# Part of the input projection by seven products for eight, ahead of the attention, in a streaming encoder layer

## The chip, the cores and the metric

The kernel runs on one core of a Trainium2 chip. The metric is the device time of one execution in microseconds (us). Engines are named as the profile names them: PE (matrix products; PEld loads its weights), DVE and ACT (elementwise work), POOL (elementwise work and some DMA issues), SP (DMA issues). SBUF is the memory on the chip that the engines read; PSUM holds the products' sums.

## The reference

One layer of an encoder for 592 rows: 64 rows of a running stream (`x_sample`, with 128 cached keys), 16 learned rows (`meta`) and 512 rows of a new stream. Group A has eight heads of differential attention, group B eight heads of latent attention.

```
h   = rmsnorm(x, norm_attn_g)
z   = h @ w_in                  # 2048 -> 3904: q 1024, k 1024, v 1024, cq 512, ckv 256, krope 64
A:  s = q_c . k_c * scale + bias (c = 0, 1);  p = softmax(s_0) - lam * softmax(s_1);  o_d = p @ v
B:  qm = rmsnorm(cq) @ w_uq;  km, vm = rmsnorm(ckv) @ w_ukv;  rotary parts;  softmax;  o_m
x   = x + concat(rmsnorm(o_d) * 0.8, o_m) @ w_out
x   = x + (silu(h2 @ w_gate) * (h2 @ w_up)) @ w_down      # h2 = rmsnorm(x, norm_ffn_g), 5632 wide
y   = rmsnorm(x, final_norm_g)
```

The new keys, values, latents and rotated keys are outputs too. Everything is float32.

## The kernel before

Columns are tokens, rows (128 partitions) are features: x is transposed once and z comes out as 31 blocks of 128 features by 592 tokens: 24 head blocks (q, k, v of heads 0 to 7), four of cq, two of ckv, one of krope written twice. A float32 number is split into a high and a low part in the format (fp32r) in which PE multiplies here (`split`: ACT makes `hi`, DVE `lo = x - hi`), and a product is three: hi.hi, lo.hi, hi.lo (`mm3`). So a block (`project`, L211) is 16 slices of the inner dimension x 3 x 2 token halves of 296 columns = 96 matmuls; its weights come in two DMAs of half a megabyte (`wr`) and are split into `wh`, `wl`.

The phases follow each other. First (L341 to L545) x is loaded token tile by token tile in four groups of columns; each of 16 chunks is transposed on PE (`transpose_x`), scaled by the norm's gain and split into `xh`, `xl`, while q and k of head 0 are already accumulated chunk by chunk, then v; DVE copies of x go to DRAM (`xspill`) for the residual sum. The row norm `rb` is multiplied in when a block is read from PSUM.

Then (to L714) the planner `Streams` (L46) interleaves generators. Each has a rank and a time at which it is ready; of those ready the lowest rank goes next, and `take`/`give` hand out PSUM banks at estimated times. Its order is binding for PE alone, whose instructions are held in program order; the other engines' are ordered by a scheduler. `projections` (rank 9) is what fills PE: q, k, v of a head, then the ckv, kr and cq blocks. Behind it run `keys`, `values` (transposes for the outputs) and `diff_attend` (L588, rank 1): for each of five query blocks and both maps (c = 0, 1) a group of score matmuls into the one bank pair `sp`, a DVE pass that adds the bias and finds the maximum (`nm`), an exponential on ACT (`e`), then the combination; then `probabilities_times_values` (L221). A head's attention starts when the one before it has ended.

Second (L717 to L991), in new rooms, `latents` turns ckv, krope and cq into keys and queries of group B (rotation, norms, splits), `latent_rows` stores the new latents, then eight latent heads run over `mix_out`, group A's half of the output projection, which fills PE. Then come the other half, and the feed-forward part, whose products are already formed by Winograd's scheme for 2 x 2 blocks (seven products and 15 sums instead of eight products), with sums of weights (`ws`) on POOL (L1112) and DVE, and sums of results (`m`) on DVE. The order of seven that this part uses is `CHAIN`; four banks a, b, c, d hold the products.

## Time and profile before

| | |
|---|---|
| median of three runs | 2491.58 us (2489.09 to 2492.69) |
| the profiled execution | 2491.91 us, span 2490.1 us, mean granted clock 0.994 |
| PE busy | 2425.4 us, 97% |
| DVE busy | 1776.4 us, 71% |
| ACT busy | 1122.4 us, 45% |
| POOL busy | 741.2 us, 30% |

All windows and rows that follow are of that profiled execution. A row of the page's groups reads: line, engine, operation, out<-in, shapes, count | total busy us, mean ns of one | idle time before them and what ended it. In a row of the timeline the first two numbers are start and duration, in us; a bracket tells an idle time before it and what ended that. A group made by a helper has the helper's line (L108 matmul, L125 the elementwise engines), so groups are told apart by their tiles' names. Busy times of matmuls overlap, because they are pipelined: what a matmul costs is the distance from one start to the next.

### The profile page before, as it was taken

Reading aid. Unit: us, or ns where it says so; the run is one execution under the profiler, and the core shown is the slowest. Engines: PE = TensorE matmul, PEld = TensorE weight load, DVE = VectorE, ACT = ScalarE, POOL = GpSimd, SP = SyncE. Lnnn points to the kernel's source line nnn. Section 1 sums busy time; section 2 is a strip of 40 time slices with the busy share of each in tenths; the row PEclk is TensorE's granted clock in tenths of the full one; section 3 lists DMA queues with packets and bytes.
Section 4 is the critical chain, followed back from the end, with each engine's and each line's share of the span. In section 5 each row is a group of like instructions: output and inputs, shape, how many; then the busy total and the mean of one; then the engine's idle time right before and its main releaser. Section 6 shows DMA issues by size and latency. Waiting matters only on the chain.

```text
span 2490.1 us, 45138 instructions
## 1 busy us (share of the span) xinstructions
PE 2425.4 (97%) x17865; PEld 2380.8 (96%) x17865; DVE 1776.4 (71%) x2815; ACT 1122.4 (45%) x2142; POOL 741.2 (30%) x598
## 2 busy tenths in 40 slices
PE   8999999998999999999999999999999999999998
PEld 6999999997999888999999999999999999999998
DVE  5555555557556467877888888888788887888874
ACT  5333333334434344445555555455554433333445
POOL 0000000001000066454554544545544422222223
PEclk9999999999999999999999999999999999999999
DMA  7433223325322454234434444344443866645332
GB/s 216 146 91 86 76 79 87 83 65 160 98 86 90 133 160 146 93 121 140 156 119 142 153 140 149 118 148 155 135 144 136 299 221 204 219 156 177 109 111 85
DMA packets 336485, 338.06 MB, mean 136 GB/s; under 512 B 25827, under 2 KB 279658, under 8 KB 336274
## 3 DMA queue, kind: packets, MB, share of 16 engines
q1 hardware_dynamic: 335714, 333.12, 41.9%
q8 instruction: 140, 2.29, 0.4%
q0 software_dynamic: 560, 2.06, 0.2%
q14 instruction: 71, 0.58, 0.1%
HBM read 265.21 MB, written 72.61 MB: 136 GB/s over the span
## 4 chain that ended last, share of the span: by engine, by line
PE 55%; DVE 2%; POOL 1%; DMA 1%; issue 1%; ACT 1%; DVEq 0%; POOLq 0%; SPq 0%
PE m L1143 36%; PE m L1147 18%; PE m L205 1%; DVE wl L125 1%; DMA raw<-in_ffn_w_down 1%; POOL ws L1112 1%; DVE b L125 0%; PE m L1510 0%; DMA raw<-in_ffn_w_gate 0%; ACT b L125 0%; DMA raw<-in_ffn_w_up 0%; DVE ws L125 0%; POOL c L1315 0%; POOL b L1497 0%; DMA b<-sumspill 0%
## 5 line engine op out<-in xcount | busy, mean ns | idle before, releaser
L1143 PE MATMUL m<-b,wh 128*128 128x288 f32 x7168 | 1048.1, 295 | 4.7 <-ACT wh L125 4.3
L1143 PEld LDWEIGHTS m<-b,wh 128*128 128x128 f32 x7168 | 983.9, 188 | 6.7 <-ACT wh L125 5.7
L1147 PE MATMUL m<-b,wl 128*128 128x288 f32 x3584 | 579.9, 297 | 2.4 <-DVE wl L125 2.2
L1112 POOL TENSOR_TENSOR ws<-raw 128x512 f32<-128x512 f32 (+1 forms) x258 | 370.4, 1445 | 543.1 <-DVE wl L125 256.5
L1147 PEld LDWEIGHTS m<-b,wl 128*128 128x128 f32 x3584 | 513.6, 188 | 4.2 <-DVE wl L125 4.1
L125 ACT ACTIVATE wh<-ws 128x512 fp32r<-128x512 f32 (+1 forms) x340 | 283.5, 846 | 391.2 <-PE m L1143 247.7
L125 DVE TENSOR_TENSOR wl<-ws,wh 128x512 fp32r<-128x512 f32 (+1 forms) x340 | 388.5, 1153 | 89.7 <-ACT wh L125 89.5
L125 DVE TENSOR_TENSOR wl<-raw,wh 128x512 fp32r<-128x512 f32 x387 | 357.3, 947 | 7.4 <-ACT wh L125 6.6
L125 ACT ACTIVATE wh<-raw 128x512 fp32r<-128x512 f32 x387 | 227.4, 620 | 286.6 <-PE m L1143 262.0
L108 PE MATMUL ps<-xh,wh 128*128 128x296 f32 x960 | 221.5, 312 | 2.3 <-ACT wh L125 2.3
L108 PE MATMUL ps<-xh,wl 128*128 128x296 f32 x960 | 210.9, 301 | 1.1 <-DVE wl L125 1.1
L108 PE MATMUL ps<-xl,wh 128*128 128x296 f32 x960 | 211.0, 301 | 0.0
L125 DVE TENSOR_TENSOR y<-y,m 128x288 f32<-128x288 f32 x312 | 139.6, 449 | 87.3 <-PE m L1147 67.9
L125 DVE TENSOR_TENSOR ws<-ws,raw 128x512 f32<-128x512 f32 (+1 forms) x129 | 114.2, 888 | 73.3 <-POOL ws L1112 71.3
L108 PEld LDWEIGHTS ps<-xh,wh 128*128 128x128 f32 x960 | 157.3, 191 | 6.8 <-ACT wh L125 3.1
L108 PEld LDWEIGHTS ps<-xh,wl 128*128 128x128 f32 x960 | 157.3, 190 | 2.1 <-DVE wl L125 2.1
L108 PEld LDWEIGHTS ps<-xl,wh 128*128 128x128 f32 x960 | 157.8, 191 | 0.0
L125 DVE TENSOR_TENSOR wl<-wr,wh 128x1024 fp32r<-128x1024 f32 (+1 forms) x110 | 118.2, 1075 | 37.3 <-ACT wh L125 35.6
L125 ACT ACTIVATE wh<-wr 128x1024 fp32r<-128x1024 f32 (+1 forms) x110 | 101.6, 929 | 63.1 <-PE ps L108 52.0
L1315 POOL TENSOR_TENSOR c<-c,rb 128x576 f32<-128x576 f32 x44 | 70.9, 1613 | 168.5 <-ACT c L125 168.5
L591 POOL MEMSET bias<- 64x64 f32 x8 | 1.2, 144 | 396.1 <-DMA bias<-tsk 231.6
L1423 POOL TENSOR_TENSOR c<-c 128x576 f32<-128x576 f32 x42 | 73.7, 1755 | 85.5 <-DVE c L125 80.3
(355 smaller groups left out, 3196.0 us busy)
## 6 DMA issues: line engine op xcount, KB each, us to landing
raw<-in_ffn_w_gate SPq DMA_DIRECT2D x44, 1024.0 KB, 7.2
raw<-in_ffn_w_up SPq DMA_DIRECT2D x44, 1024.0 KB, 6.8
raw<-in_ffn_w_down SPq DMA_DIRECT2D x39, 1024.0 KB, 5.4
partspill<-parts SPq DMA_DIRECT2D x126, 288.0 KB, 2.1
b<-partspill SPq DMA_DIRECT2D x126, 288.0 KB, 5.9
wr<-in_w_in SPq DMA_DIRECT2D x60, 512.0 KB, 4.1
wr<-in_w_out SPq DMA_DIRECT2D x16, 512.0 KB, 4.4
wr<-in_w_out SPq DMA_DIRECT2D x32, 256.0 KB, 3.6
```

Source lines behind the costliest of these rows:

```text
L108: self.tc.keep_in_program_order(self.pe.matmul(out, lhsT, rhs, start=start, stop=stop))
L125: ins = issue(*args, **kwargs)
L205: PE.matmul(outs[i], w, x[i], start=start and p == 0, stop=stop and p == 2)
L591: G.memset(bias[0:64, 464:528], -BIG)
L1112: engine.tensor_tensor(w[:, k:k + m, :], pick(xs), pick(ys), op=op)
L1143: PE.matmul(banks[p], wh[:, k, :], x, start=first and new and k == 0 and x is hi, stop=False, skip_group_check=not new)
L1147: PE.matmul(banks[p], wl[:, k, :], hi, start=False, stop=last and k == n - 1, skip_group_check=not new)
L1315: G.tensor_tensor(g[:, f, :], g[:, f, :], rb2, op=ALU.mult)
L1423: G.tensor_tensor(w[:, f, :], w[:, f, :], g[:, f, :], op=ALU.mult)
```

## The change

Three parts.

*Seven products for eight.* A block pair is seen as 2 x 2: token halves by feature halves of 128, and the inner 2048 split into even and odd chunks. Of the 31 blocks, 17 are projected first, before any attention: q and k of heads 0, 1, 2 (`EARLY`), the eight v in pairs, the two ckv, each pair as a `Product` of 7 x 24 matmuls, and kr as a `Single` of 4 x 24. x is loaded whole, transposed, copied with the gain (`xg`) and without (`xt`, to `xspill`, now whole rows), and the operands of the seven products are built from `xg`: four kinds in rooms that last as x's splits (p = 1, 2, 3, 5) and three others (6, 7, 4). Two pairs run interleaved at first (`START`, in the written order of DVE, ACT and SP too), then the others one behind the other (`run`). The norm `rb` is computed behind them from x loaded once more. The results go to DRAM (`zspill`).

*Heads overlap.* `heads` (rank 5) loads q, k, v of a head again and multiplies by `rb` on POOL where that is due; `projections` (rank 9) has only the q and k of heads 3 to 7 and cq left, 14 blocks, each now in two PSUM tiles of one bank. A head's scores start after the scores of the head before; the two maps have a bank each (`s0`, `s1`), the wide block 3 takes both; the transposes have two banks; probabilities (`pt_b`) have two sets, `e` four, `p5` two.

*Latents in x's room.* The key latents' norm (`key_latents`) runs at the start of the attention. With the last projection x's room (`xk`) is closed and `latents` is spawned in a new pool in that place, so the cosines, the rotation, the queries' norm and the row stores run before the phase ends, and the latent heads start with the next phase at once.

The diff, cut to its core:

```diff
+EARLY = 3
...
-    def project(ps, wsrc, xs, dup=False):
-                mm3([ps[:, 0, 0:TH], ps[:, 1, 0:TH]], wh[:, k, :], wl[:, k, :],
-                    halves(xs[kc][0]), halves(xs[kc][1]), kc == 0, kc == KC - 1)
+    def project(ps, wsrc, xs):
+                for h in ((0,), (1,)) if kc == 0 else ((0, 1),):
+                    mm3([ps[i][:, 0:TH] for i in h], wh[:, k, :], wl[:, k, :],
+                        [hi[i] for i in h], [lo[i] for i in h], kc == 0, kc == KC - 1)
...
+            def transpose_x(kc):
+                cg, k = kc // 4, kc % 4
+                ps = banks()
+                for j, (o, n) in enumerate(tok):
+                    b = o // TH
+                    PE.transpose(ps[:, b, o - b * TH:o - b * TH + n],
+                                 xt_in[cg, j][0:n, k * P:(k + 1) * P], ident[0:n, 0:n])
+                xg[kc] = room((7, 4)[kc % 2], kc // 2)
+                S.activation(xg[kc], ev(ps), AF.Copy, scale=gA[:, kc:kc + 1])
+                xt[kc] = room((6, 5)[kc // 8], kc % 8)
+                V.tensor_copy(xt[kc], ev(ps))
+            def split_operand(p, m, src):
+                t = room(p, m, F32R)
+                operands[p, m] = ends(t)
+                split(*operands[p, m], src)
+            def first_operands(m):
+                (b11, b12), (b21, b22) = ends(xg[2 * m]), ends(xg[2 * m + 1])
+                split_operand(1, m, b11)
+                split_operand(2, m, b21)
+                G.tensor_tensor(b11, b12, b11, op=ALU.subtract)
+            def other_operands():
+                for m in range(PAIRS):
+                    split_operand(3, m, xg[2 * m + 1][:, 1, :])
+                    yield
+                def sums(n):
+                    t = flat(wp.tile([P, 8, P], F32, name="wr", tag="wr", bufs=WR_BUFS))
+                    return [t[:, i * TH:(i + 1) * TH] for i in range(n)]
+                for m in range(PAIRS):
+                    if m % 3 == 0:
+                        c = sums(3)
+                    G.tensor_tensor(c[m % 3], xg[2 * m + 1][:, 1, :], xg[2 * m][:, 0, :], op=ALU.subtract)
+                    split_operand(6, m, c[m % 3])
+                    yield
+                for m in range(PAIRS):
+                    split_operand(5, m, xg[2 * m][:, 0, :])
+                    yield
+                for m in range(PAIRS):
+                    (t5, b12), (b21, b22) = ends(xg[2 * m]), ends(xg[2 * m + 1])
+                    c7, c4 = sums(2)
+                    G.tensor_tensor(c7, b22, b12, op=ALU.subtract)
+                    G.tensor_tensor(c4, b21, b22, op=ALU.subtract)
+                    G.tensor_tensor(c4, c4, t5, op=ALU.add)
+                    split_operand(7, m, c7)
+                    yield
+                    split_operand(4, m, c4)
+                    yield
+            class Product:
...
+                def weights(self, p, early=False):
+                    a11, a12, a21, a22 = (self.a[f, t] for f in range(2) for t in range(2))
+                    if p == 5:
+                        self.sum = src = self.combine(G, a21, a22, ALU.add, self.sum)
+                    elif p == 6:
+                        src = self.sum if early else self.combine(V, self.sum, a11, ALU.subtract, self.sum)
+                    elif p == 3:
+                        if early:
+                            self.sum = self.combine(G, a21, a22, ALU.add)
+                            self.combine(V, self.sum, a11, ALU.subtract, self.sum)
+                        src = self.combine(V, a12, self.sum, ALU.subtract, a12 if early else self.sum)
+                    elif p == 7:
+                        src = self.combine(G, a11, a21, ALU.subtract, a11)
+                    else:
+                        src = {1: a11, 2: a12, 4: a22}[p]
+                    wh = wp.tile([P, 8, P], F32R, name="wh", tag="wh", bufs=WH_BUFS)
+                    wl = wp.tile([P, 8, P], F32R, name="wl", tag="wl", bufs=WH_BUFS)
+                    for i, x in enumerate(src):
+                        split(wh[:, 4 * i:4 * i + 4, :], wl[:, 4 * i:4 * i + 4, :], x)
+                    return wh, wl
+                def multiply(self, p, name, w, first):
+                    wh, wl = w
+                    out = {"a": self.ab[:, 0, 0:TH], "b": self.ab[:, 1, 0:TH],
+                           "c": self.c_[:, 0, 0:TH], "d": self.c_[:, 1, 0:TH]}[name]
+                    self.bank[p] = out
+                    for m in range(PAIRS):
+                        for x in operands[p, m]:
+                            PE.matmul(out, wh[:, m, :], x, start=first and m == 0 and x is operands[p, m][0],
+                                      stop=False, skip_group_check=not first)
+                    for m in range(PAIRS):
+                        PE.matmul(out, wl[:, m, :], operands[p, m][0], start=False, stop=m == PAIRS - 1,
+                                  skip_group_check=not first)
...
+                def run(self, chain, step):
+                    seen = set()
+                    for p, name in chain:
+                        self.multiply(p, name, self.weights(p), name not in seen)
+                        seen.add(name)
+                        self.take(p)
+                        step()
+                    self.keep()
...
+            load_x(0)
+            load_x(1)
+            load(oh, c_onehot)
+            load(rbt, rel_bias)
+            raws = [raw_weights((0, P), (OFF_K, P))]
+            load_x(2)
+            load_x(3)
+            raws.append(raw_weights((P, P), (OFF_K + P, P)))
...
+            first, second = [Product(r, (h, 8 + h)) for h, r in enumerate(raws)]
+            START = [(1, "a", first), (2, "c", first), (1, "a", second), (2, "c", second)]
+            START += [(p, n, c) for p, n in ((3, "d"), (6, "a"), (5, "b"), (7, "a"), (4, "a")) for c in (first, second)]
+            ws = [c.weights(p, True) for p, n, c in START[:2]]
+            for kc in range(KC):
+                store(xspill[kc], flat(xt[kc]))
+            store(trow, trs)
+            building = other_operands()
+            for _ in range(PAIRS):
+                next(building)
+            for i, (p, name, call) in enumerate(START):
+                call.multiply(p, name, ws.pop(0), p not in (6, 7, 4))
+                call.take(p, True)
+                for _ in range(3 + i % 2):
+                    next(building, None)
+                if i + 2 < len(START):
+                    q, _, c = START[i + 2]
+                    ws.append(c.weights(q, True))
...
+            for h in range(2, EARLY):
+                Product(raw_weights((h * P, P), (OFF_K + h * P, P)), (h, 8 + h)).run(CHAIN, step)
+            for h in range(0, H, 2):
+                Product(raw_weights((OFF_V + h * P, 2 * P)), (16 + h, 17 + h)).run(CHAIN, step)
+            Product(raw_weights((OFF_CKV, 2 * P)), (28, 29)).run(CHAIN, step)
+            last = raw_weights((OFF_KR, 64), (OFF_KR, 64))
+            Single(last, (30,)).run(((1, "a"), (2, "c"), (6, "a"), (3, "b")), step)
...
-                    yield from st.take("sp")
-                    n, W, view, vw = scores(b, sbig(), [qs[h % 2][c]], [(kh, kl)])
+                    if b == 3:
+                        sp = yield from take_both()
+                    else:
+                        yield from st.take(f"s{c}")
+                        sp = sbanks[:, c:c + 1, :]
+                    n, W, view, vw = scores(b, sp, [qs[h % 2][c]], [(kh, kl)])
...
+        def projections():
+            for i in [o + h for h in range(EARLY, H) for o in (0, 8)]:
+                ps = pjt()
+                off = i * P if i < 8 else OFF_K + (i - 8) * P
+                yield from project(ps, w_in[:, off:off + P], xs1)
+                z = ztile()
+                normed(z, ps)
+                store(zspill[i], z)
+                projected[i]["done"] = True
+            for i in range(4):
+                off = OFF_CQ + i * P
+                ps = pjt()
+                yield from project(ps, w_in[:, off:off + P], xs1)
+                z = ztile()
+                normed(z, ps)
+                store(zspill[24 + i], z)
+            xk_cm.__exit__(None, None, None)
+            st.spawn(4, latents())
+        def projected_rows(i, z):
+            load(z, zspill[i])
+            if not (EARLY <= i < 8 or 8 + EARLY <= i < 16):
+                G.tensor_tensor(z, z, rb, op=ALU.mult)
+            return z
+        def heads():
+            for h in range(H):
+                yield [projected[h], projected[8 + h]] + ([scored[h - 2]] if h >= 2 else [])
+                zq = projected_rows(h, ztile())
+                if h >= 1:
+                    yield [nat[2 * h - 1], nat[2 * h - 2]]
+                zk = projected_rows(8 + h, ztile())
+                yield 4.0
+                for c in range(2):
+                    r = slice(c * DH, (c + 1) * DH)
+                    split_scaled(qs[h % 2][c][0][r, :], qs[h % 2][c][1][r, :], zq[r, :], DH ** -0.5)
+                kh = ap.tile([P, TP], F32R, name="kh", bufs=2)
+                kl = ap.tile([P, TP], F32R, name="kl", bufs=2)
+                split(kh[:, 0:T], kl[:, 0:T], zk)
+                nat[2 * h] = st.spawn(2, keys(h, zk, kh, kl))
+                if h >= 2:
+                    yield [att[h - 2]]
+                zv = projected_rows(16 + h, ztile())
+                yield 2.0 if h == 0 else 4.0
+                vh = ap.tile([P, 6, P], F32R, name="vh", bufs=2)
+                vl = ap.tile([P, 6, P], F32R, name="vl", bufs=2)
+                nat[2 * h + 1] = st.spawn(2, values(h, zv, vh, vl))
+                att[h] = st.spawn(1, diff_attend(h, kh, kl, vh, vl), [keyed[h]] + ([scored[h - 1]] if h else []))
+        for name, n in (("s0", 1), ("s1", 1), ("tp", 2), ("po", 1)):
+            st.bank(name, n)
+        st.spawn(5, heads())
+        st.spawn(9, projections())
+        st.spawn(4, key_latents())
...
-        first = st.spawn(0, latents())
-        rows = st.spawn(1, latent_rows(), [first])
-        st.spawn(20, heads(), [first])
+        st.spawn(20, heads())
```

More of the change, by code (lines that the diff above doesn't have):

```diff
@@ L313, in hv, with rotate @@
         return t[:, 0:n].rearrange("p (a b) -> p a b", a=2)
+    def rotate(dst, z, pr, t, own):
+        for i in range(2):
+            PE.matmul(pr[:, i, 0:TH], own.rot, z[:, i * TH:(i + 1) * TH], start=True, stop=True)
+        V.tensor_tensor(hv(t), ev(pr), hv(own.sin), op=ALU.mult)
+        G.tensor_tensor(dst, z, own.cos, op=ALU.mult)
+        V.tensor_tensor(dst, dst, t, op=ALU.add)
     def sum_squares(pq, tiles, tile_of):
@@ L519, in encoder_step @@
-            V.tensor_scalar(g08, g08, 1.0 - LAM_INIT, None, op0=ALU.mult)
-            for h in range(H):
-                Q.dma_start(tsk[h], trow[h:h + 1, :].to_broadcast([P, NREL]))
-        for e in (V, S, Q):
-            e.ordered = False
+                    PE.matmul(pb[:, b, o - b * TH:o - b * TH + n], rc[0:n, j:j + 1].to_broadcast([n, P]),
+                              ident[0:n, 0:n], start=True, stop=True)
+                V.tensor_copy(hv(rb), ev(pb))
+                yield
+            background = norm()
@@ new lines, in step @@
+            def step():
+                next(background, None)
+            for h in range(2, EARLY):
[4 more added lines that the diff above has]
+            last = raw_weights((OFF_KR, 64), (OFF_KR, 64))
+            for m in range(PAIRS):
+                operands[0, m] = hi, lo = ends(room(5, m, F32R))
+                load(f32(lo), xspill[2 * m, :, TH:T])
```

617 lines of the change are left out of this document (305 added, 312 removed).

## The prediction

> **What bounds the kernel now.** I read the page first (busy shares, slices), then the view of busy time by window, whose edges I put where the first value block of head 0 ends (78), where the last projection ends (559.6), where the latent heads start to run evenly (606), and round a stretch of the feed-forward part.
>
> ```profile
> span 2490.1 us, 45138 instructions
> PE 2425.4 (97%) x17865; PEld 2380.8 (96%) x17865; DVE 1776.4 (71%) x2815; ACT 1122.4 (45%) x2142; POOL 741.2 (30%) x598
> 0.00:78.00 78.00, 66.01 (x415) 56.73 (x416) 43.94 (x82) 41.06 (x88) 5.15 (x17) 1.00 0.75 222
> 78.00:559.60 481.60, 471.97 (x3436) 462.25 (x3435) 262.91 (x565) 181.19 (x376) 1.01 (x7) 0.99 0.30 84
> 559.60:606.00 46.40, 35.56 (x206) 30.68 (x206) 36.96 (x54) 23.05 (x37) 10.03 (x21) 0.89 0.63 188
> 1058.00:1120.00 62.00, 62.00 (x469) 62.00 (x468) 47.94 (x54) 26.47 (x42) 32.60 (x24) 1.00 0.37 122
> ```
>
> A window's row gives its edges, its length, busy time and count of PE, weight loads, DVE, ACT and POOL, then TensorE's granted clock, DMA's share and GB/s. TensorE is the bound (97%), so the change is worth what TensorE no longer has to do, less what it waits more. Only in 0:78 and 559.6:606 is it plainly short of work. A matmul step of 288 columns costs 62.00/469 = 0.132 us where nothing is missing; of 296 columns 0.132 x 296/288 = 0.136. A block of 96 such matmuls is then 13.05 us.
>
> **The change, part by part.** All is compared at the point where the handover to the latent heads begins (before: 559.6).
>
> *Products.* Sixteen blocks (q and k of heads 0 to 2, eight v, two ckv) go in eight pairs, 7 x 24 = 168 matmuls for 192: 22.85 us a pair instead of 26.1. The saving is 8 x 24 = 192 matmuls, 26.1 us. Its price is a start in which nothing is multiplied until all of x is there, and more sums on DVE and POOL.
>
> *The start.* x lands last in the new order too: the bytes queued ahead are the same, 592 x 2048 numbers of x (4.85 MB) and head 0's q and k weights (2.1 MB).
>
> ```profile
> 28.20 4.18 SPq L125 DMA_DIRECT2D xn<-in_x_prompt  x5
> DMA to landing us min/median/max: 2.5/5.5/9.6
> L125 DVE COPY xt<-pxt 128x592 f32<-128x592 f32 x8 | 6.1, 763 | 0.0
> L125 DVE TENSOR_TENSOR b<-b 128x288 fp32r<-128x288 f32 x22 | 13.0, 607 | 0.0
> L125 DVE TENSOR_TENSOR b<-xg,b 128x288 fp32r<-128x288 f32 x24 | 22.7, 968 | 9.1 <-ACT b L125 9.1
> L125 DVE TENSOR_TENSOR wl<-raw,wh 128x512 fp32r<-128x512 f32 x381 | 353.5, 952 | 7.4 <-ACT wh L125 6.6 <-PE m L1147 0.8
> L125 DVE TENSOR_TENSOR wl<-ws,wh 128x512 fp32r<-128x512 f32 x168 | 128.8, 787 | 1.1 <-ACT wh L125 0.9
> L125 DVE TENSOR_TENSOR ws<-ws,raw 128x512 f32<-128x512 f32 x127 | 112.4, 888 | 73.3 <-POOL ws L1112 71.3
> L125 DVE TENSOR_TENSOR ws<-raw,ws 128x512 f32<-128x512 f32 x127 | 84.8, 695 | 0.9
> L125 DVE TENSOR_TENSOR c<-c,m 128x288 f32<-128x288 f32 x172 | 73.5, 447 | 15.5 <-ACT wh L125 8.6 <-PE m L1147 6.8
> L1112 POOL TENSOR_TENSOR ws<-raw 128x512 f32<-128x512 f32 x254 | 366.8, 1453 | 539.7 <-DVE wl L125 253.1 <-DMA raw<-in_ffn_w_down 95.9 <-ACT wh L125 50.1
> L1054 POOL TENSOR_TENSOR bs<-xg,bs 128x288 f32<-128x288 f32 x8 | 6.7, 833 | 3.5 <-DVE b L125 2.7 <-DMA x<-x1spill 0.8
> ```
>
> (The second row is the landing time of the x tiles; a group's row gives total busy, then the mean ns of one.) The last five x loads are issued from 28.2 to 32.4 and land by about 34. DVE then still has two pairs, 2 x (2 x 0.763 + 2 x 0.607) = 5.5, so the first product starts near 40. From there DVE, not TensorE, sets the pace: up to the ninth of the fourteen products it does 14 weight halves from raw (13.3), 8 from sums (6.3), 39 operand splits at 0.607 (23.7), weight sums 4 x 0.888 + 4 x 0.695 (6.3), five additions of results (2.2) and lambda's small ones (1, an estimate): 52.8. Four more products on TensorE are 4 x 3.26 = 13.1. The start ends at S = 40 + 52.8 + 13.1 = 106. Bounds: 87 were TensorE the only limit (40 + 45.7, and 1.5 for the first weights), 120 if the 39 splits take 0.968 each. I take 106: 0.607 is the row of a split without a second pass over xg. The sixteen whole stores of x on SP and the stores' release of rooms lie inside this; ACT's part of a split, being shorter than DVE's, too.
>
> *From S to the last projection.* The raw weights of head 2 wait for the two buffers that the first product's last weights free: 1.5 us (0 to 5). Six pairs take 137.1; kr, 4 x 24 matmuls, 13.05. Then rooms are swapped and the first heads' q and k, loaded back, are multiplied by rb on POOL, behind eight fills of rooms:
>
> ```profile
> L1189 POOL TENSOR_TENSOR sq<-sq,rb 128x576 f32<-128x576 f32 x15 | 23.2, 1545 | 1.2
> L125 DVE TENSOR_TENSOR wl<-wr,wh 128x1024 fp32r<-128x1024 f32 x78 | 95.3, 1222 | 32.6 <-ACT wh L125 31.5
> L125 DVE TENSOR_TENSOR z<-ps,rb 128x592 f32<-128x592 f32 x15 | 11.6, 773 | 15.1 <-PE ps L108 15.1
> ```
>
> I take 4 us there (2 to 8): a multiplication of 1.5, ACT and DVE behind it, while projections of head 3 already fill TensorE. The fourteen blocks left take 182.7. The twelve squares of the norm run on ACT during the pairs, and 2 MB of weights in 22.85 us is 92 GB/s, near the 84 shown before: no charge. TensorE's attention work is what remains before of 481.6 after 28 blocks (365.4): 116.2, or 14.5 a head with its waits. Sum without a change in waits: 106 + 1.5 + 137.1 + 13.05 + 4 + 182.7 + 116.2 = 560.6, against 559.6: +1.0. So the start eats the 26.1.
>
> *Waits inside a head.* Before, all ten score groups share one bank pair, and the last block's two are short:
>
> ```profile
> 294.00:298.00 4.00, 2.27 (x21) 1.94 (x20) 3.96 (x11) 3.15 (x7) 0.08 (x1) 0.92 0.30 78
> 299.00:303.00 4.00, 4.00 (x26) 3.98 (x26) 1.77 (x7) 0.98 (x3) 0.00 (x0) 0.78 0.31 84
> 295.21 0.28 PE L108 MATMUL sp<-kh,q10h 128*64 128x128 f32 x1 [0.81 <-DVE nm L125]
> 296.67 0.28 PE L108 MATMUL sp<-kh,q11h 128*64 128x128 f32 x1 [0.92 <-DVE nm L125]
> 297.44 0.69 PE L108 MATMUL ps<-xl,wh 128*128 128x296 f32 x2
> 297.93 0.69 PE L108 MATMUL ps<-xh,wl 128*128 128x296 f32 x2
> ```
>
> TensorE waits 0.81 and 0.92 us for DVE to read the bank, and the steps after that start 0.245 us apart (297.44 to 297.93 for two) instead of 0.136 for some ten matmuls (window 299:303: clock 0.78). Together up to 1.7 + 10 x 0.11 = 2.8 a head. The change gives each of the two maps a bank and lets heads overlap, so these two groups stand back to back behind thirty projection matmuls. But there is half the fill: DVE was busy 262.9 of 481.6 (55%); it loses 28 x (2 x 1.222 + 0.773) = 90 and gains 14 x 3.4 = 48 (a block's two weight halves and two half-width products), some 220 in about 291 (76%), as much as the 47.94 of 62 at which the feed-forward part keeps TensorE full. I take 1 us a head net, 8 in all (between a gain of 2.8 and a loss of 1.7 a head).
>
> A rule speaks on this. The Trainium skill, "TensorE: Matmul & The Clock Gate", Part 1, has the half clock come only after an idle window of about 3.4 us. By it two gaps under 1 us cost just themselves, and the gain is at most 1.7 a head; the rows 297.44 and 299:303 show the slow steps after those gaps all the same, so the measurement decides.
>
> *Handover.* Before, TensorE is filled badly while rotation, key latents and queries' norm run one behind the other:
>
> ```profile
> 559.70 0.34 SPq L125 DMA_DIRECT2D mspill<-o  x1
> 563.03 1.77 PE L108 MATMUL pr<-zl,rot 128*128 128x296 f32 x4 [3.32 <-DMA rot<-c_rot]
> 569.53 0.45 PE L112 MATMUL pkr<-ident,rn 128*128 128x128 f32 x1 [4.73 <-ACT mxh L125]
> 584.56 0.54 PE L108 MATMUL ps<-cqh,mh 128*128 128x296 f32 x2 [0.47 <-DVE v L125]
> ```
>
> 206 matmuls in 46.4 us leave about 15 unused at the granted clock. Now the last projection spawns this chain ahead of head 7's last values. It starts earlier, but with head 7's values as its only cover; on SP the queries' weights are issued behind rot, cos, sin, the cq loads, the row stores and head 7's result, and the first latent q product must wait for them, about 21 us after the last projection. I charge 0, with 5 gained and 6 lost as bounds. Afterwards the work is the same; the residual rows now come in pieces by SP beside 113 us with spare DMA: 0.
>
> *Sum.* +1.0 - 8 + 0 = -7 against the profiled execution, 2491.91 us (span 2490.1), which agrees with the median of 2491.58 to 0.02%: 2485.
>
> **The rivals.**
>
> A, a slower start. POOL makes 32 operand sums (26.7) and 12 halves of weight sums (17.4) in the start, 44 us beside DVE. If DVE's splits then take 0.968 each instead of 0.607, S is 106 + 39 x 0.36 = 120 and the time 2499: slower. It decides from S = 118, 12 above the forecast's. For it: the two rows of b, 968 and 607, of the same shape. Against: in 1058:1120 DVE's 47.94 and POOL's 32.60 sum to 80.5 in 62 us, so at least 18.5 us ran side by side. The Trainium skill, "SBUF — State Buffer", "Who interferes with whom", calls the port pair of the two engines an exclusive lock held for a whole instruction; by it the 44 us could all be added, 2529, and the overlap just shown does not agree with that in full.
>
> B, attention bound by DVE. With half the fill, the score groups of blocks 0 to 3 wait as the last ones do now: two more waits of 0.81 and 0.92 a head, and none of the present ones gone. That is 8 x 1.7 = 14 more and the 8 not gained: 2507. It decides from a loss of 0.6 a head. For it: 76% DVE busy on average, in bursts. Against: overlapping heads, and two banks.
>
> C, no change. The products that DVE paces leave TensorE at steps of 0.245, 5.9 us a product, and of the last four, which I took at 3.26, three are still slow: 3 x 2.6 = 8, S = 114, 2493. For it: row 299:303, slow after gaps under 1 us. Against: the steady 0.132 of the feed-forward part, which is fed by the same kinds of sums.
>
> D, better. ACT's, DVE's and TensorE's work interleaves so well that S is 96 to 97 (of the bounds 87 and 106, the middle), the two waits of a head go whole (1.7 in place of 1, 8 x 0.7 = 5.6), and the handover gains 3: 2485 - 9.5 - 5.6 - 3 = 2467. For it: DVE's 52.8 counts sums that could be made before x is complete. Against: ACT and POOL feed each of them.
>
> **How the numbers follow.** Forecast (2475 to 2487) 0.32, A 0.20, B 0.17, C 0.13, D 0.18. Within 0.2%, 5 us, is about what a measurement of this kernel cannot tell from no change. Faster: forecast and D, 0.50; same: C, 0.13; slower: A and B, 0.37. The range runs from below D's centre, 2463, to past B's, 2513.
>
> **What would show it.** In the profile after: the first product's matmul near 40; the last product of the second pair ending near 106, with DVE near full between (A: 120; C: granted clock under 0.9 there); pairs 22.85 apart, no gap over 2 us between them; the last projection ending with attention work at about 553; score groups without the two waits of about 0.9; first latent q product 21 us behind the last projection's end. It would be wrong by a pair spaced over 23.5 (DVE- or DMA-bound products), by score groups waiting on `nm` in every block (B), or by a hole over 10 us at the room swap near 260.

## The result, and the profile after

The changed kernel takes 2607.77 us (median; 2605.97 to 2609.43) against 2490.91 us (2489.09 to 2492.69): 1.0469 times as long, interval 1.0451 to 1.0487. Slower by 117 us, where 2485, about 6 us faster, was forecast.

The page of the changed kernel (span, busy shares, slices; the helpers' lines are L111 for matmuls and L128 for the elementwise engines there), and then its busy time by window, cut where the start ends (120.5), kr ends (306), head 7's last values end (660) and the second half of the output projection begins (970.5; before: 855.9):

```profile
span 2607.1 us, 45453 instructions
PE 2446.9 (94%) x17673; PEld 2386.0 (92%) x17673; DVE 1888.4 (72%) x2986; ACT 1190.1 (46%) x2298; POOL 865.5 (33%) x697
PE   6788888889699989999999999999999999999998
DVE  6855576666555545787787888888888888888874
...
0.00:120.50 120.50, 87.18 (x438) 74.16 (x439) 83.63 (x131) 54.52 (x116) 60.51 (x57) 0.87 0.56 166
120.50:306.00 185.50, 162.69 (x1117) 156.81 (x1116) 102.91 (x149) 76.88 (x149) 36.98 (x25) 0.97 0.40 124
306.00:660.00 354.00, 308.87 (x2107) 290.11 (x2105) 232.46 (x541) 153.63 (x351) 35.55 (x46) 0.96 0.38 111
660.00:970.50 310.50, 276.09 (x1984) 262.85 (x1983) 172.25 (x328) 123.86 (x266) 15.90 (x44) 0.95 0.33 100
```

The same window of the kernel before, from the last projection to the second half of the output projection:

```profile
559.60:855.90 296.30, 276.00 (x1984) 261.09 (x1983) 175.46 (x333) 120.09 (x262) 19.17 (x48) 0.98 0.34 103
```

TensorE executes 192 matmuls fewer, as planned (17673 for 17865), and is idle more: 94% for 97%. The idle time lies mainly in the first nine of the forty slices and in the eleventh (652 to 717), which read 6 to 8 where nearly all read 9 before. Against the forecast's terms the start takes 120.4 instead of 106 (+14), the six pairs and kr 185.5 instead of 151.7 (+34), the attention with the swap of rooms 354 instead of 294.9 (+59), the stretch behind it 310.5 instead of 296.3 (+14), what follows 1636.6 instead of 1634.2 (+2): 124 us if summed before rounding, which is the distance of the profiled execution (2607.1 us and 1.8 around it) from the forecast.

Two views tell what the first two of the large terms are. The first is a pair of value blocks in the timeline; the second a block of scores of head 2, both of the changed kernel:

```profile
216.11 0.40 ACT L128 ACTIVATE c<-m 128x296 f32<-128x296 f32 x1
216.56 2.45 PE L111 MATMUL m<-b,wh 128*128 128x296 f32 x16 [1.47 <-ACT c L128]
220.61 2.46 PE L111 MATMUL m<-b,wh 128*128 128x296 f32 x16 [0.53 <-ACT c L128]
223.99 2.37 PE L111 MATMUL m<-b,wh 128*128 128x296 f32 x16
231.37 2.42 PE L111 MATMUL m<-b,wh 128*128 128x296 f32 x16 [0.65 <-DVE c L128]
235.51 2.41 PE L111 MATMUL m<-b,wh 128*128 128x296 f32 x16 [0.65 <-DVE c L128]
```

```profile
414.11 0.27 PE L111 MATMUL sp<-kh,q00l 128*128 128x144 f32 x1
414.62 0.29 DVE L128 CUSTOM_DVE_ANT_0 e<-sp,bias 128x144 f32<-128x144 f32 x1
414.97 0.33 PE L111 MATMUL sp<-kh,q01h 128*128 128x144 f32 x1 [0.59 <-DVE nm L128]
```

And from the view of waits (total, times, longest), of the changed kernel in 307 to 655 and of the kernel before in 78 to 560:

```profile
PE sp L111 <- DVE nm L128: 33.4, 33, 2.3
PE sp L108 <- DVE nm L125: 8.4, 9, 1.6
```

The product at 216.56 is the second of its pair and goes into bank b; it waits for the copy out of bank a, made at 216.11. The scores of the second map, into bank `s1`, wait until DVE has read the first map's out of `s0`. Of seven products, four wait so, and are those that follow a product in the other half of the same tile of two banks (`self.ab`); the product into c, another tile, does not wait. The same for the two halves of `sbanks`.

### The profile page after: what moved, and what is told of

The parts are those of the page before. It is cut to its first block, busy times and chain, and to the rows that moved or that the text cites. A ratio compares the mean times of both kernels' runs of the same rounds, so it can differ in the third digit from the quotient of the medians.

```text
span 2607.1 us, 45453 instructions
## 1 busy us (share of the span) xinstructions
PE 2446.9 (94%) x17673; PEld 2386.0 (92%) x17673; DVE 1888.4 (72%) x2986; ACT 1190.1 (46%) x2298; POOL 865.5 (33%) x697
## 4 chain that ended last, share of the span: by engine, by line
PE 55%; DVE 1%; POOL 1%; DMA 0%; ACT 0%; issue 0%; DVEq 0%; POOLq 0%; SPq 0%; ACTq 0%
PE m L1359 36%; PE m L1363 18%; PE m L208 1%; DVE b L128 0%; PE m L1726 0%; DVE wl L128 0%; DMA raw<-in_ffn_w_down 0%; ACT b L128 0%; POOL b L1713 0%; DMA b<-actspill 0%; ACT y L128 0%; POOL b L1708 0%; PE m L1740 0%; DVE y L128 0%; POOL sq L1405 0%
## 5 line engine op out<-in xcount | busy, mean ns | idle before, releaser
L1359 PEld LDWEIGHTS m<-b,wh 128*128 128x128 f32 x7168 | 984.1, 189 | 7.4 <-ACT wh L128 5.3
L128 DVE TENSOR_TENSOR wl<-ws,wh 128x512 fp32r<-128x512 f32 (+1 forms) x386 | 433.9, 1138 | 108.7 <-ACT wh L128 104.3
L128 ACT ACTIVATE wh<-ws 128x512 fp32r<-128x512 f32 (+1 forms) x386 | 310.2, 819 | 428.4 <-PE m L1359 256.8
L128 ACT ACTIVATE wh<-raw 128x512 fp32r<-128x512 f32 (+1 forms) x461 | 270.2, 621 | 359.8 <-PE m L1359 258.4
L128 DVE TENSOR_TENSOR wl<-raw,wh 128x512 fp32r<-128x512 f32 (+1 forms) x459 | 409.9, 921 | 33.0 <-PE m L111 20.2
L128 DVE TENSOR_TENSOR y<-y,m 128x288 f32<-128x288 f32 x312 | 140.1, 450 | 88.2 <-PE m L1363 68.0
L111 PE MATMUL m<-b,wh 128*128 128x296 f32 x960 | 157.6, 321 | 42.5 <-ACT wh L128 19.7
L111 PEld LDWEIGHTS m<-b,wh 128*128 128x128 f32 x960 | 146.2, 206 | 49.9 <-ACT wh L128 31.6
L128 DVE TENSOR_TENSOR ws<-ws,raw 128x512 f32<-128x512 f32 (+1 forms) x145 | 130.2, 905 | 68.0 <-POOL ws L1328 65.5
L111 PE MATMUL ps<-b,wh 128*128 128x296 f32 x896 | 175.4, 317 | 2.1 <-DVE z L128 1.4
L111 PEld LDWEIGHTS ps<-b,wh 128*128 128x128 f32 x896 | 140.2, 198 | 7.0 <-DVE z L128 3.8
L128 DVE TENSOR_TENSOR c<-c,m 128x288 f32<-128x288 f32 (+1 forms) x200 | 86.6, 450 | 56.0 <-PE m L111 35.9
L111 PE MATMUL ps<-b,wl 128*128 128x296 f32 x448 | 102.8, 307 | 0.0
L128 ACT ACTIVATE parts<-c 128x1 fp32r<-128x1 f32 x252 | 81.2, 322 | 37.1 <-DVE c L128 30.5
L128 DVE TENSOR_TENSOR wl<-wr,wh 128x1024 fp32r<-128x1024 f32 (+1 forms) x76 | 84.4, 1110 | 16.6 <-ACT wh L128 15.1
L128 DVE TENSOR_TENSOR ws<-raw,ws 128x512 f32<-128x512 f32 (+1 forms) x141 | 94.4, 698 | 0.9
```

Source lines behind the costliest of these rows:

```text
L111: self.tc.keep_in_program_order(self.pe.matmul(out, lhsT, rhs, start=start, stop=stop, **kwargs))
L128: ins = issue(*args, **kwargs)
L1359: PE.matmul(banks[p], wh[:, k, :], x, start=first and new and k == 0 and x is hi, stop=False, skip_group_check=not new)
```

## The experiments

Where no range or interval is given, an experiment is a single run. Four runs of one version lie 3 to 8 us apart here, so a difference under about 5 us between single runs says little.

**One bank, one tile, for the products.**

```diff
-                    self.ab, self.c_ = banks(), banks()      # two tiles of [P, 2, 512]
+                    self.own[name] = pq1.tile([P, 512], F32, name="m", tag="m1")   # a, b, c, d each
```

> Only this differs from the changed kernel: a product's banks a, b, c, d are four tiles of one bank each instead of two tiles of two banks. Theory (a tile of two banks is waited for as one thing, so a product into bank b waits until the copy out of bank a is done): the four gaps of 0.8 to 0.95 us in each pair go, the last four pairs take 22.9 to 23.5 us instead of 26.2 to 27.2, kr's start comes 16 to 30 us earlier, and the time is 2577 to 2591. Rival (the gaps are the late weights, ACT and DVE in order): pairs stay at 26 to 27, time within 5 us of 2608.

Measured: 2575.6 us, 32 less. The projections behind kr begin at 278.4 instead of 307.0. The pairs in the timeline of this kernel, product by product:

```profile
215.37 2.35 PE L111 MATMUL m<-b,wh 128*128 128x296 f32 x16
217.56 1.25 PE L111 MATMUL m<-b,wl 128*128 128x296 f32 x8
218.65 2.34 PE L111 MATMUL m<-b,wh 128*128 128x296 f32 x16
...
235.02 2.35 PE L111 MATMUL m<-b,wh 128*128 128x296 f32 x16
237.21 1.25 PE L111 MATMUL m<-b,wl 128*128 128x296 f32 x8
238.29 1.93 PE L111 MATMUL m<-b,wh 128*128 128x296 f32 x13
```

A product starts each 3.27 to 3.28 us without a gap (238.29 - 215.37 = 22.92 for seven), close to the forecast's 22.85. So the gaps were the tile and not late weights. It also shows what they had cost: with them a pair took 26.2 to 27.2 us, as much as the 26.1 of the eight products that it replaces.

**One bank, one tile, for the scores, and the other way round: the old order on the shared tile.**

```diff
-        sbanks = pss.tile([P, 2, 512], F32, name="sp")
+        sbanks = [pss.tile([P, 512], F32, name="sp", tag=f"sp{i}") for i in range(2)]
```

> Only this differs from the changed kernel: the score banks s0 and s1 are two tiles of one bank instead of one tile of two (block 3, whose groups take both, reads them with two DVE operations and a small minimum; the norms' sums are read in two halves). Theory (one tile is waited for as one): TensorE's waits of score groups for nm fall from 33.4 us to under 9, slow steps after them too, the attention stage shortens by 25 to 45 us, time 2563 to 2583. Rival (DVE is too late for the scores with half the fill): the waits appear in front of the next groups, gain under 10 us.

```diff
-                    if b == 3 and c == 0:
-                        yield 2.0
+                    if c == 0:
+                        yield 2.0 if b == 3 else 1.2 + 0.0015 * W
```

> Only this differs from the changed kernel: after the first map's scores the planner waits 1.2 us and more, as before the change, so projection matmuls stand between the two maps' groups; the banks stay one tile. Theory (order planned for banks that are independent, on banks that are not): waits for nm fall from 33.4 to under 12 us, time 2570 to 2588. Rival (DVE too late): gain under 10 us. Were own tiles much better than this, it is the tile that matters; were both alike, the order.

Measured: own tiles 2571.79 us, 36 less; the order alone 2597.44, 10 less. Here are the waits of the first in 306 to 615, then two windows of the second:

```profile
PE sp L111 <- DVE nm L128: 1.5, 1, 1.5
```

```profile
306.00:580.00 274.00, 261.33 (x1884) 252.25 (x1885) 187.39 (x417) 120.95 (x269) 29.39 (x39) 0.98 0.44 129
580.00:680.00 100.00, 61.20 (x260) 44.96 (x259) 63.43 (x155) 48.19 (x110) 10.22 (x22) 0.68 0.31 97
```

With own tiles the waits for `nm` all but go. With the old order on the shared tile they go too (7.7 us in ten waits), but the projections that stand between the two maps are then used up at 580, 75 us early, and the last heads run with nothing to fill TensorE: 61 of 100 us busy, clock 0.68. So the waits fell as expected (under 12), and the time did not (2570 to 2588): the old order takes away the wait only by spending fill, and fourteen blocks are not enough for that. It does not show DVE to be too late.

**The multiplications by rb on DVE.** In the timeline of the changed kernel, where kr has ended and the first heads' rows come back:

```profile
306.81 1.22 DVE L128 TENSOR_TENSOR wl<-wr,wh 128x1024 fp32r<-128x1024 f32 x1
314.55 4.21 POOL L997 TENSOR_TENSOR kz<-kz,rb 128x592 f32<-128x592 f32 x3
314.59 9.46 DVE L128 TENSOR_TENSOR wl<-wr,wh 128x1024 fp32r<-128x1024 f32 x1 [6.57 <-ACT wh L128]
318.73 4.24 POOL L997 TENSOR_TENSOR z<-z,rb 128x592 f32<-128x592 f32 x3
```

```diff
-                G.tensor_tensor(z, z, rb, op=ALU.mult)
+                V.tensor_tensor(z, z, rb, op=ALU.mult)
```

> Only this differs from the changed kernel: the rows of heads' q, k, v and key latents that are loaded back are multiplied by rb on DVE, not on POOL. Theory (a DVE operation that reads two tiles in SBUF stands still while POOL's runs: at 314.6 us one weight split takes 9.46 us instead of 1.22, beside six multiplications of 1.4 on POOL): the split there falls to 1.3, the stretch from kr's end to the first scores gets 6 to 10 us shorter, time 2596 to 2603. Rival (the split waits for something else, and nine more operations on DVE cost as much as they free): time 2604 to 2612.

Measured: 2599.69 us, 8 less, and the stretch in this kernel's timeline:

```profile
316.48 2.16 DVE L128 TENSOR_TENSOR kz<-kz,rb 128x592 f32<-128x592 f32 x3 [5.36 <-DMA kz<-zspill]
319.01 1.22 DVE L128 TENSOR_TENSOR wl<-wr,wh 128x1024 fp32r<-128x1024 f32 x1 [0.38 <-ACT wh L128]
```

The weight split that needs 1.22 us alone stood for 9.46 beside six multiplications on POOL, and ends 1.1 us behind the last of them, about as long as it takes alone; with POOL out of the way it is 1.22 again, and the multiplications take 0.72 to 0.77 each on DVE instead of 1.4. This is what the Trainium skill, "SBUF — State Buffer", "Who interferes with whom", calls an exclusive lock of the port pair of DVE and GpSimd; here the trace agrees. From the first projection behind kr to the first scores are 16.1 us (310.0 to 326.2) instead of 22.1 (307.0 to 329.0).

**The start.** Three runs ask what sets its 120.4. First POOL's 32 operand sums left out, with tiles that are there already split in their place, so that products 6, 7 and 4 are made of other operands:

```diff
-                    G.tensor_tensor(c[m % 3], xg[2 * m + 1][:, 1, :], xg[2 * m][:, 0, :], op=ALU.subtract)
-                    split_operand(6, m, c[m % 3])
+                    split_operand(6, m, f32(operands[3, m][0]))     # and so for products 7 and 4
```

> POOL's 32 sums for the operands of products 6, 7 and 4 are left out; the operands are split from tiles that are there already (so those three products are not the right ones). All else as changed. Theory (the start is set by POOL's sums and by ACT's and DVE's queues standing behind them in the written order): the start's last product ends at 100 to 109 instead of 120.4, and the time falls by 10 to 20 us. Rival (DVE's own work or TensorE at half clock sets it): it ends after 115.

then the sums on DVE (`G.tensor_tensor` to `V.tensor_tensor` in the four lines of `other_operands`):

> Only this differs from the changed kernel: the 32 operand sums of the start run on DVE, not on POOL. Theory (POOL's sums hold DVE still and the written order holds ACT and DVE behind POOL): on DVE they cost 32 x 0.45 = 14 us at most, the start ends at 105 to 114 instead of 120.4, time 2594 to 2602. Rival (DVE is the limit of the start by its own work, 61 of 67 us): it ends at 125 to 134, time 2612 to 2622.

and, on top of three gains (below), the weights written ahead of the operands' splits:

```diff
+                if i + 2 < len(START):
+                    q, _, c = START[i + 2]
+                    ws.append(c.weights(q, True))
                 for _ in range(3 + i % 2):
                     next(building, None)
-                if i + 2 < len(START):
-                    q, _, c = START[i + 2]
-                    ws.append(c.weights(q, True))
```

> As the run with the three gains, but in the start the weights of the product after next are written ahead of the next operands' splits, so that on ACT and DVE they stand before the splits that wait for POOL. Theory (order): the start ends at 108 to 114 instead of 120.5, time 6 to 12 us less than with the three. Rival (the sum of DVE's and POOL's work): it ends at 118 or later.

Measured: without the sums the start ends at 101.8 and the time is 2589.88; with the sums on DVE it ends at 125.6, 2618.26; with the weights first at 119.7, 2537.22 (with the three gains alone 120.7 and 2535.84). The windows from 41 to the start's end, of the changed kernel, without the sums, and with the sums on DVE, in this order:

```profile
41.00:120.40 79.40, 60.31 (x336) 58.12 (x337) 64.63 (x95) 35.54 (x83) 49.46 (x43) 0.81 0.38 126
```

```profile
41.00:102.00 61.00, 52.09 (x337) 50.74 (x338) 54.86 (x95) 39.80 (x92) 20.64 (x14) 0.94 0.60 199
```

```profile
41.00:125.60 84.60, 62.00 (x335) 59.52 (x336) 69.15 (x126) 35.74 (x82) 20.92 (x14) 0.84 0.36 118
```

The sums cost 18.6 us where they are and 24 on DVE; the order alone changes nothing. In the changed kernel the products come late up to 107.3, and from there four follow each other without a gap. Here are that stretch, three groups of DVE in it, and a wait of ACT:

```profile
41.00:107.30 66.30, 47.23 (x240) 45.04 (x240) 57.31 (x82) 27.21 (x67) 48.06 (x42) 0.77 0.30 110
L128 DVE TENSOR_TENSOR b<-wr,b 128x296 fp32r<-128x296 f32 x23 | 16.1, 732 | 8.5 <-ACT b L128 8.5
L128 DVE TENSOR_TENSOR b<-b,b 128x296 fp32r<-128x296 f32 x18 | 9.0, 557 | 0.0
L128 DVE TENSOR_TENSOR raw<-raw,ws 128x512 f32<-128x512 f32 x4 | 6.8, 1750 | 0.0
ACT b L128 <- POOL wr L480: 14.3, 6, 4.6
```

DVE is busy for 57.3 of 66.3 us; of the rest it waits 8.5 for ACT's half of an operand split, and ACT waits for POOL's sums. Without the sums DVE is busy for 46.9 of 47.8 us in the same stretch (41 to 88.8). With the sums on DVE it is ACT that waits for DVE's sums (32.5 us in 41 to 112.6), and DVE again for ACT (8.4): the chain of sum, high part and low part stays. Beside POOL, DVE's operations are long too, as two rows of the changed kernel's timeline show:

```profile
64.89 3.38 POOL L501 TENSOR_TENSOR raw<-raw 128x512 f32<-128x512 f32 x2
65.39 3.42 DVE L128 TENSOR_TENSOR raw<-raw,ws 128x512 f32<-128x512 f32 x2
67.92 4.32 PE L111 MATMUL m<-b,wh 128*128 128x296 f32 x16 [4.32 <-ACT wh L128]
```

Two sums of weights take 3.42 us on DVE where one took 0.695 in the rows before; TensorE then waits 4.3 us for weights that ACT splits behind them, and the 16 matmuls after that wait take 4.32 us for 2.4.

**The handover.** The first latent q product waits 12 us for its weights, queued behind the row stores:

```profile
680.22 0.69 PE L115 MATMUL pn<-ident,kz 128*128 128x128 f32 x2 [3.84 <-DVE nn L128]
684.95 3.92 POOL L1039 DMA_DIRECT2D mxl<-mspill  x7 [24.61 <-DMA out<-nn]
693.26 0.83 PE L111 MATMUL ps<-cqh,mh 128*128 128x296 f32 x2 [12.06 <-DMA mr<-in_mla_w_uq]
```

```diff
+            own.first = [l2.tile([P, 4, 2, 64], F32, name="m0")]     # loaded at the start of latents()
```

> Only this differs from the changed kernel: the weights of the first rotary queries are loaded ahead of the latents' other loads instead of behind the row stores, head 7's result and its reload. Theory (the first latent q product waits 12.1 us for that load alone): it starts at 681 to 684 instead of 693.3; since the next weights still come late, 4 to 9 us of it remain at the end, time 2599 to 2604. Rival (the output projection's fill, which comes at 698, and not the weights ends the hole): the product starts earlier, the time stays within 3 us of 2608.

Measured: the product starts at 686.7, the time is 2610.12: nothing gained, as the rival had it. The product's fill, `mix_out`, cannot start without `mxl`, whose first load goes out at 685.9 there and at 684.4 in the changed kernel. All that was known taken away together:

> All causes taken away together: single-bank tiles for the products and for the scores, rows multiplied by rb on DVE, operand sums of the start on DVE, the first rotary weights early. If they are separate and each is worth what it is alone (32, 36, about 8, about 10, about 6 us), the time is 2508 to 2522, still slower than before by 0.7 to 1.2%. If one hides another: over 2530. Under 2500 would need a gain that no single run shows.

Measured: 2539.36 us (ratio to before 1.019, 1.0173 to 1.0207), not 2508 to 2522, since two of the five are no gains: the single results, 32, 36 and 8 less, 10 and 2 more, would make 2544. Without those two:

> Single-bank tiles for products and for scores, and the rows multiplied by rb on DVE; the start and the handover as in the change. If the three gains add (32, 36, 8): 2530 to 2535, 4 to 9 us better than with the sums on DVE and the early weights too. Still slower than before by 1.6%.

Measured: 2535.84 us (1.0177, 1.0157 to 1.0197). The single gains would make 2531.5, so the three add to within 4 us, which is no more than the spread. On this base two further runs ask about the handover: head 7's sums ahead of the latents' (`yield [att[H - 1]]` before `take_both` in `latents`):

> As the run with the three gains, but the latent part asks for the score banks for the sums of the queries' norm only after head 7 has ended. Theory (head 7's last sums stand 14 us behind the latents' 16 sums, its result is stored at 682, and as the rooms of the output projection lie where the attention's were, its loads and the fill wait for that): the first fill matmul comes 6 to 12 us earlier than in the run with the three, time 4 to 10 us less. Rival (the fill is held by something else): no change, within 3 us.

Measured: 2539.02 us, nothing. Head 7's sums start 6.3 us earlier (596.2 for 602.6) and its result is stored 2.2 us earlier (608.2 for 610.4), but the last row transpose comes 4.4 us later (612.9 for 608.5), and the loads of `mxl` come right behind that (613.8 for 612.6). Then the row transposes as a stream right behind the rotation:

```diff
+            rows = st.spawn(3, latent_rows())        # behind rotate(kr, ...); body as before
...
-            for j in range(5):                       # behind the queries' norm
+            yield [rows]
```

> As the run with the three gains, but the five transposes of the latent rows (which read the key latents out of the attention's rooms) run as a stream of their own right behind the rotation, not behind the queries' norm. Theory (these rooms come free only with the last of the transposes, at 608.9, and the loads of the output projection's operands go out right behind, at 612.6): loads and fill come 4 to 8 us earlier, time 3 to 8 us less than with the three (2528 to 2533). Rival (the loads wait for another thing): within 3 us.

Measured: 2527.31 us (1.0149, 1.0133 to 1.0164), 8.5 less. The last row transpose, the store of head 7's result, the first load and the first fill, with the three gains and then with the rows first:

```profile
608.45 0.44 PE L115 MATMUL pn<-ident,kz 128*128 128x128 f32 x2 [3.64 <-DVE nn L128]
610.39 0.39 SPq L128 DMA_DIRECT2D mspill<-o  x1
612.62 0.33 SPq L1071 DMA_DIRECT2D mxl<-mspill  x1
627.11 0.42 PE L111 MATMUL ps<-mxh,wh 128*128 128x288 f32 x2
```

```profile
595.49 0.66 PE L115 MATMUL pn<-ident,kz 128*128 128x128 f32 x2 [3.46 <-DVE nn L128]
599.79 0.33 SPq L128 DMA_DIRECT2D mspill<-o  x1
601.96 0.33 SPq L1076 DMA_DIRECT2D mxl<-mspill  x1
616.19 0.43 PE L111 MATMUL ps<-mxh,wh 128*128 128x288 f32 x2
```

The transposes read the key latents `kz`, which lie in the attention's rooms, and so does head 7's result `o`; the output projection's operands get these rooms, and one of them is that result, read back. In these traces the loads come right behind the later of two things. In both blocks, as in the changed kernel (682.2 and 684.4), the first load goes out 2.2 us behind the store of head 7's result, and the view of SP's waits names that store; the last transpose starts 4 us and more ahead of the load. In the run before this, with head 7 first, it was the transpose. Rows first brought both forward, the transpose by 13.0 us and the store by 10.6, and the loads moved by 10.7. Before the change the store went out at 559.7, as the last projection ended, and the loads from 562.0 on. The early weights on top:

> Rows first and the first rotary weights early, both. Theory (the late weights, 12.6 us of wait, and the late fill hide each other, so that each alone shows nothing or little): together 8 to 14 us less than with the three, 2522 to 2528. Rival (separate, weights worth nothing): as with rows first alone.

Measured: 2528.89 us (1.0156, 1.0139 to 1.0173): nothing more that shows beside the spread of its runs (2522.74 to 2530.98).

**How many heads ahead**, with the three gains, `EARLY = 2` and `EARLY = 4`:

> As the run with the three gains, but only heads 0 and 1 are projected ahead (EARLY 2): one pair of products less (+3.3 us of matmuls), two blocks more as fill for the attention. If what is left of the waits in the attention comes from too little fill (DVE too late for 14 blocks): time 3 to 10 us less than with the three. If not: 2 to 5 us more.

> The other side: heads 0 to 3 ahead (EARLY 4), 12 blocks of fill. If fill is what lacks: 5 to 20 us more than with the three. If TensorE's matmuls alone count: 2 to 5 us less.

Measured: 2536.84 and 2552.05 us. Between two heads and three the difference of 1 us cannot be told from the spread (2532.21 to 2537.68 with three), so neither a loss nor the 3.3 us of a pair's matmuls is shown; from three to four it costs 16: with twelve blocks of fill the projections end at 561, and the attention goes on to 614. In that window of the last kernel:

```profile
561.00:616.00 55.00, 38.87 (x167) 29.64 (x166) 36.99 (x95) 29.95 (x66) 4.01 (x5) 0.76 0.30 91
```

No version here beats the kernel before; the best is 1.5% behind it.

## Why the prediction was wrong

*Waits inside a head: this step failed.* "The change gives each of the two maps a bank": I took this to mean that each can be written while the other is read. The two banks are halves of one tile and are waited for as one. The planner had them as two, so it put the second map's scores right behind the first's: the projection matmuls that used to stand between them, and hid the wait, were gone. The forecast gained 8 us; 33.4 us of waits for `nm`, for 8.4 before, were the outcome, and slow steps after them (granted clock 0.96 in 306 to 660; before, 0.99 in 78 to 559.6). Own tiles brought 36 us. Rival B had the sign and the place (the score groups of blocks 0 to 3 waiting as the last did), but not the cause: DVE was in time once the tiles were split. Not even with twelve blocks of fill do the score groups wait for DVE (one wait of 0.8 us in 250 to 616); what is missing there is fill, with DVE busy for 37 of 55 us. A small misreading besides: in the kernel before, the slow steps behind the two waits were fourteen (297.05 to 300.40), not ten, so that 2.8 a head should have been 3.2.

*Products: the same mistake.* The term 22.85 is right for a pair (22.92 without the shared tile) and was mis-sized as the kernel stood: 26.2 to 27.2, and 30 to 34 for the first two pairs. I had the bank names a, b, c of the scheme in view and did not ask in how many tiles they lie. The feed-forward part, from which I took the step, holds each bank in a tile of its own. Together with the start this takes away all of what the sixteen blocks were to save.

*The start: the 52.8 us of DVE, measured 66.2.* The forecast had DVE as the limit, and DVE never waiting. From the first product (41.1) to the last four (107.3) it was busy for 57.3 us and idle for 9.0, nearly all of it behind ACT, which waited for POOL's sums; that is the larger part. Of the 4.5 more busy time most is sums of weights, 10.6 for 6.3, and the halves made from them, 8.9 for 6.3. The operand splits, 25.1 us for 41, cost what was assumed (23.7 for 39). So rival A had the place, POOL beside DVE, and its number, 120 for a measured 120.4, was luck: its price was 0.968 a split, and the splits did not pay it. C's sign, a granted clock under 0.9, appears as well (0.77), but not in the last four products, where C put its price (13.2 us for 13.1): five of the first ten products took 4.2 to 4.3 us in their first sixteen matmuls instead of 2.4, four of them after waits of 3.2 to 4.5 us. How much of the start these slow steps cost by themselves is not shown. Gaps of 0.8 to 1.6 us between the later products were followed by steps at full speed; the row at 297.44 in the kernel before, from which C was drawn, follows two gaps amid short matmuls. For gaps like those of the pairs the trace agrees with the rule that I set aside (the Trainium skill, "TensorE: Matmul & The Clock Gate", Part 1). It does not where a wait of 2.07 us (to 88.48) was followed by sixteen matmuls in 3.44.

*Room swap: 4 us was too little.* I priced six multiplications on POOL as work beside other work. They held DVE, and through it TensorE: moving them gave 8 us in a single run, 6 of them ahead of the first scores. The rule on the port pair (the Trainium skill, "SBUF — State Buffer", "Who interferes with whom"), which I had set aside because 18.5 us of the feed-forward part showed both engines busy, fits here; busy at the same time is not the same as running at the same time, since an operation that stands still counts as busy.

*Handover: charged 0, cost 14.* The first latent q product came 39 us behind the last projection where 21 were expected, but bringing it forward gave nothing. The price lay in what I had left out: the loads for the output projection come only behind the store of head 7's result and the last transpose of the rows. Before, that store went out as the last projection ended; now both stand amid the latents' work, the store 22 us behind head 7's last values (660 to 682.2). 8.5 us of it are shown, by moving the rows, which brought both forward.

What holds: the 192 matmuls saved, the first product near 40 (41.1), and next to no loss in the feed-forward part (+2). Left of the 117 us in the best version are 36: some 15 where kr ends, which is mostly the start (17 blocks at 275.3, where 78 + 14 x 13.05 = 260.7 would be the pace of before), 12 in the attention, 6 in the handover, 3 behind it. The last three are not traced further.

## What to carry to other kernels

Before counting on two banks, look in how many tiles they lie: here a wait was for a tile, and a planner that counts banks then puts dependent work back to back. When an elementwise step is moved to POOL to relieve DVE, price it on DVE too wherever DVE reads two operands in SBUF at that moment; but measure before moving it back, since the six multiplications gained 8 us on DVE and the 32 sums lost 10. And when the inputs of a later stage get the rooms of an earlier one, the last reader in the old rooms, here the store of head 7's result or a few transposes for an output, sets when the later stage may load.

## What the runs showed of the hardware

One DVE operation that reads two tiles in SBUF stayed 9.46 us instead of 1.22 while six POOL operations ran one behind the other: it did not get in between them, though it stood ready at the start of the first. And TensorE kept its full step after isolated idle stretches of up to 1.5 us in the changed kernel (the pairs), while stretches of 3.1 to 4.5 us were followed by sixteen matmuls in 4.0 to 4.3 us instead of 2.4, and one of 2.07 by 3.44. There is no sharp bound in between: with the three gains a wait of 3.10 us (to 88.63) was followed by 2.43, one of 2.64 (to 101.56) by 4.32.
